# Hybrid recurrent decoder, two layers: a K 1024 product run out and back, S5 phases packed over partition halves, stores moved to GpSimd

## The chip, the core and the metric

The kernel runs on one core of a Trainium2 chip. The metric is the device time of one execution in microseconds. Timed runs and one profiled execution are given; the profiled one has a trace of every instruction.

## What is computed

Two layers of a decoder trunk for 512 prompt tokens and 64 sample tokens (8 sequences of 8), 576 columns in all, width 1024, in float32. Per layer:

```
h = RMSNorm(x);  P = h @ W_in                 (columns for four mixers and four gates)
A retention (4 heads), B Mamba-2 SSD (8 heads), C HGRN2 (4 heads), D S5 (32 groups of 16, 64 complex states)
m = sum_b sigmoid(P_gate_b) * (o_b @ W_branch_b);   x = x + RMSNorm(m @ W_out)
x = x + RMSNorm(relu(RMSNorm(x) @ W_1)^2 @ W_2)     (hidden width 4096)
```

It returns the outputs of both groups and the new recurrent states of every mixer (retention, SSD, convolution rows, HGRN2, S5), for each layer.

## The kernel before

Activations are kept transposed: features on the 128 partitions, tokens as columns, in two halves of 256 and 320 columns. Every dense product is made of three float32r products, (hi + lo) x (hi + lo) without lo x lo: `mm3` issues three matmuls for each 128 rows of K. A weight block (512 KB) is loaded by the SP queue into one of three `raw` buffers; ScalarE rounds it to `whi`, VectorE subtracts to get `wlo` (`wblock`), each in one of four buffers. So a fifth block is split only when TensorE has done with the first.

`dense` takes its output tiles in groups of four blocks. For a group it loads four blocks and runs all of its tiles for half 0, then all for half 1 (`order`). `hooks` are functions called ahead of a given tile of the last group: they put the norm of a half that is ready among the products that are still to run. `dense_turn` runs a first set of four tiles for half 0, the next set for half 0 and then half 1, and loads the first set again for half 1; it joins one product to the next, when half 1 of the input is not ready yet.

After the out-projection (`out_proj`, 8 tiles, K 1024, two groups) come `post` (norm of the result, added to `x`) and `norm` (the input of the FFN), for each half: squares on ScalarE, their sums and the scaling on VectorE, the sum over partitions on TensorE. `HK` places them: half 0's at tiles 0, 1 and 2 of half 1 in the last group, half 1's at tiles 1, 2 and 5 of the FFN's `dense_turn`. The FFN (`ffn`) takes the hidden width in eight chunks of 512: `up(c)` makes the chunk (relu, square, split into hi and lo), and the second product adds it into `y`, with K 512 and two tiles to a block. With the eighth chunk of layer 0 come the post-norm and layer 1's first norm, at the places `HM` and, for half 1, at `HN` in the `dense_turn` of layer 1 (four S5 tiles, then four of retention's first head).

S5 is run from tables that `s5_build` makes once per layer, on VectorE for the most part: groups of 16 channels in eight steps of four (`o`), each with an input table (`m2`), an output table (`cw`) and phases (`ph`, powers of the complex decay over 64 steps, from the power tables `w` and `E`), stored to DRAM (`tabd`) and loaded later. The 64 states stand on the partitions twice, as rows 0 to 63 and 64 to 127. Layer 0's tables are made beside the first mixer (retention), layer 1's beside layer 0's last merge. The places come from `SCHED`, a string with one letter per step, written out by hand.

All new states are stored by the SP queue, which also carries every load. A queue runs in order: a store waits there for its data, and what is behind it waits too. GpSimd has 16 memsets (HGRN2's `at` and `ats`) and four constants to write, and nothing else.

The order within an engine is made when the kernel is built: a planner goes through the operations with a cost model and gives each engine the ready operation that stands first in the written program; a buffer's next user waits for the last use of the one before. What the hardware does later than the plan thought, it does in that order still.

Of the kernel before, what the change touches and what calls it, by code (L numbers as in the profile page):

```python
# [40 lines left out]
FP = (0,4,7)  # L41
HN = (1,4,5)
HK = (0,1,2,1,2,5)
HM = (0,4,6)
HL = (0,5)
# [4 lines left out]
class Kernel:  # L50
# [586 lines left out]
    def out_proj(self, l, p, m, x):  # L637

        w = self.io["w_out"][l]
        y = [self.ytile(hf, "y") for hf in range(2)]  # L640
        h = []

        def take(k):
            return lambda ps, hf: self.act(y[hf][:, k], ps)

        post = lambda hf: lambda: self.post(y[hf], hf, p["g_post_mix"], x)
        norm = [self.norm(x, hf, p["g_pre_ffn"], "h", h) for hf in range(2)]
        step = lambda hf: lambda: next(norm[hf], None)
        self.dense(w, [(128 * k, take(k)) for k in range(8)], m, hooks=self.hooks(HK[:3], post(0), step(0), 1))
        return h, self.hooks(HK[3:], post(1), step(1))  # L650
# [11 lines left out]
    def ffn(self, l, p, h, rest, x, nxt, u1):  # L662
# [34 lines left out]
        if nxt is None:  # L697
            rows, done = self.last_rows(x[0], y[0], p["g_post_ffn"]), [0, 4]

            def tiles(k=None):  # L700

                if k is None:
                    self.store_x(x, 1)
                    done[1] = 8
                else:
                    done[0] += 1
                while done[1] and done[0]:
                    next(rows)
                    done[0] -= 1
                    done[1] -= 1  # L710
            order, hooks, end = (1, 0), {(0, HL[0]): [post(1)], (0, HL[1]): [tiles]}, None
        else:
            order, hooks = (0, 1), self.hooks(HM, post(0), step(0), 1)
            end = self.hooks(HN, post(1), step(1))
# [4 lines left out]
        for c in range(8):  # L719
            if c == 7 and nxt is None:  # L720
                next(rows)
            if c > 1:
                us.append(up(c))
                self.dense(w1, us[c][1], h)
            u = us[c][0]
            ua = [[(u[hf][0][:, i], u[hf][1][:, i]) for i in range(4)] for hf in range(2)]
            jobs = [(128 * k, take2(c, k)) for k in range(8)]
            if c < 7:
# [183 lines left out]
    def mixer_ret(self, l, p, h, res, turn):  # L912
        out, wi = [], self.io["w_in"][l]
        for hd in range(4):
# [26 lines left out]
            g = GAMMA[hd]  # L941
# [25 lines left out]
            for c in range(1, 4):  # L967
                self.stt(S[:, c], S[:, c - 1], g ** 128, pu[:, 128 * c:128 * c + 128], OP.mult, OP.add)
            self.nc.sync.dma_start(self.io["ret_prompt"][l, 0, hd], S[:, 3])

# [39 lines left out]
    def mixer_hg(self, l, p, h, res):  # L1010
        out, wi = [], self.io["w_in"][l]
        for hd in range(4):
# [107 lines left out]
            self.nc.sync.dma_start(self.io["hgrn_prompt"][l, 0, hd], S[:, 3])  # L1120
            o, sq = self.f([128, T], name="o"), self.f([128, T], name="osq")
# [16 lines left out]
            for i in range(2):  # L1138
                ps = self.pm()
                self.outer(ps, kts, vm[i])  # L1140
                for b in range(4):
                    c = NP + 8 * (4 * i + b) + 7
                    self.stt(st[i][:, b], st[i][:, b], eg[:, c:c + 1], ps[:, 128 * b:128 * b + 128], OP.mult, OP.add)
                self.nc.sync.dma_start(self.io["hgrn_sample"][l, 4 * i:4 * i + 4, hd].rearrange("b d e -> d b e"), st[i])
            rs = self.rowstat([sq], 1.0 / 128)
# [116 lines left out]
    def mixer_ssd(self, l, p, h, res):  # L1262
# [12 lines left out]
        for g in range(2):  # L1275
# [26 lines left out]
            for pr in range(2):  # L1302
# [29 lines left out]
                self.act(sp, ps[:, :128])  # L1332
                nc.sync.dma_start(io["ssd_prompt"][l, 0, h0:h0 + 2].rearrange("h p n -> (h p) n"), sp)

# [49 lines left out]
                for i in range(2):  # L1384
                    ps = self.pm()
                    self.outer(ps, xes, vm[i])
                    for b in range(4):
                        self.stt(st[i][:, b], st[i][:, b], dt["esm"][:, q, 4 * i + b:4 * i + b + 1],
                                 ps[:, 128 * b:128 * b + 128], OP.mult, OP.add)
                    nc.sync.dma_start(io["ssd_sample"][l, 4 * i:4 * i + 4, h0:h0 + 2].rearrange("b h p n -> (h p) b n"), st[i])  # L1390
            sq = [self.f([128, T], name="ssq") for _ in range(2)]
# [7 lines left out]
        for q in range(2):  # L1399
# [4 lines left out]
            self.act(r, ps[:27])  # L1404
            nc.sync.dma_start(io["conv_prompt"][l, 0][:, 512 * q:512 * q + 512], r[:3])
            nc.sync.dma_start(io["conv_sample"][l].rearrange("b r f -> (b r) f")[:, 512 * q:512 * q + 512], r[3:])
        self.dump(f"o_ssd{l}", out)
# [13 lines left out]
    def s5_build(self, l):  # L1421
# [3 lines left out]
        if l == 0:  # L1425

            A = self.slots.tile([128, 2048], F32, name="s5ba", tag="yA", bufs=1)
            Bt = self.slots.tile([128, 2560], F32, name="s5bb", tag="yB", bufs=1)
            base = [A[:, 512 * i:512 * i + 512] for i in range(4)] + [Bt[:, 512 * i:512 * i + 512] for i in range(2)]
            w, t, dd = Bt[:, 1024:1472], Bt[:, 1472:1984], Bt[:16, 1984:2496]  # L1430
        else:
            base = [self.f([128, 512], name="s5base") for _ in range(6)]
            w, t, dd = (self.f([128, n], name="s5t") for n in (448, 512, 512))
            dd = dd[:16]
# [19 lines left out]
        for i, (c, n) in enumerate(zip(C, ("s5_c_re", "s5_c_im"))):  # L1454
# [13 lines left out]
        t4 = t[:, :128].rearrange("p (k g) -> p k g", k=4)  # L1468
        for e, k0 in ((E[1], 0), (E[0], 3)):
            self.V.memset(e[:, 0, 0], 1.0)  # L1470
            self.V.memset(e[:, 0, 1], 0.0)
            for k in range(3):
                n = 1 << k
                self.cmulb((e[:, n:2 * n, 0], e[:, n:2 * n, 1]), (e[:, :n, 0], e[:, :n, 1]),
                           (w[:, k0 + k:k0 + k + 1, 0].to_broadcast([128, n, 32]),
                            w[:, k0 + k:k0 + k + 1, 1].to_broadcast([128, n, 32])), t4[:, :n])
        C3 = [g3(c) for c in C]
# [3 lines left out]
        for o in range(8):  # L1481
# [21 lines left out]
            self.tt(cw, cw, tmp, OP.add)  # L1503
            ph4 = v(ph, "p (c g a b) -> p c g a b", c=2, g=4, a=8)
            ea = lambda c: E[0][:, :, c, gs].rearrange("p a g -> p g a")[:, :, :, None].to_broadcast([128, 4, 8, 8])
            eb = lambda c: E[1][:, :, c, gs].rearrange("p b g -> p g b")[:, :, None, :].to_broadcast([128, 4, 8, 8])
            self.cmulb((ph4[:, 0], ph4[:, 1]), (ea(0), ea(1)), (eb(0), eb(1)), v(tm3, "p (g a b) -> p g a b", g=4, a=8))
            yield
# [10 lines left out]
            self.dq.dma_start(self.taps[l][:, 4 * o:4 * o + 4, 128:], kt[:16].rearrange("p (g q) -> p g q", g=4))  # L1519
            for (b0, b1, _, _), t in zip(self.TABS, (m2, cw, ph)):  # L1520
                self.dq.dma_start(self.tabd[l, o, :, b0:b1], t)
            if o == 7:

# [33 lines left out]
    def mixer_s5(self, l, p, ud):  # L1557
# [121 lines left out]
        for c, n in enumerate(("s5_re", "s5_im")):  # L1679
            nc.sync.dma_start(io[n + "_sample"][l].rearrange("(i b) g p -> (b g) i p", i=2), r[:, :2, 64 * c:64 * c + 64])  # L1680
            nc.sync.dma_start(io[n + "_prompt"][l, 0], r[:32, 2, 64 * c:64 * c + 64])
        self.dump(f"o_s5{l}", out)
# [78 lines left out]
```

## Time and profile before

| | |
|---|---|
| median of 3 timed runs | 2729.14 us (2728.92 to 2735.39) |
| the profiled execution | 2728.35 us, span of its instructions 2726.5 us |
| TensorE (PE) busy | 2651.0 us, 97% |
| VectorE (DVE) busy | 1735.4 us, 64% |
| ScalarE (ACT) busy | 1155.4 us, 42% |
| GpSimd (POOL) busy | 5.2 us |
| moved by DMA | 278.95 MB, mean 102 GB/s |

A row of the profile names the line of the kernel, the engine, the operation and the tiles (output <- inputs). Where a helper issues an operation, the line is the helper's, so tiles tell more: L108 is every matmul, L90 every ScalarE operation, L93 every two-operand VectorE operation. `pd` is the PSUM of dense products, `pm` that of all others. "SPq" is the SP queue, issuing or waiting.

### The profile page before, as it was taken

To read this page: it belongs to the slowest core of one execution; us is meant where nothing else is said; L and a number is where in the kernel's file an instruction comes from. 1 tells how busy PE (TensorE), PEld (TensorE's weight loads), DVE (VectorE), ACT (ScalarE), POOL (GpSimd) and SP (SyncE) were. 2 spreads that over 40 slices of the span, in tenths; PEclk is the share of its full clock that TensorE was granted. 3 is DMA by queue.
4 is the path that set the end of the run, shared out by engine and by line. 5 is a ranking of instruction groups with operands and counts; after the bars stand their busy time and mean duration, and the time that the engine had idled before them with its cause. 6 is when DMAs were issued, how large, how long until landed. Compare 5 with 4: busy or idle time off the path is not lost.

```text
span 2726.5 us, 48170 instructions
## 1 busy us (share of the span) xinstructions
PE 2651.0 (97%) x19498; PEld 2580.0 (95%) x19498; DVE 1735.4 (64%) x3806; ACT 1155.4 (42%) x2233; POOL 5.2 (0%) x20
## 2 busy tenths in 40 slices
PE   8989999999998999999989999999999999999998
PEld 8878999999998989999989999999999999999998
DVE  7797677867769483444485567777767546444445
ACT  5444554543532363322354554544434335423223
POOL 0000000000000000000000000000000000000000
PEclk9998999999999999999999999999999999999999
DMA  6445333332543533223244343333334323322221
GB/s 192 111 146 146 96 99 90 84 103 77 144 102 125 172 86 101 74 82 93 73 117 119 81 107 94 89 94 107 95 92 133 117 76 90 97 86 77 86 86 51
DMA packets 450540, 278.95 MB, mean 102 GB/s; under 512 B 58344, under 2 KB 430626, under 8 KB 449294
## 3 DMA queue, kind: packets, MB, share of 16 engines
q1 hardware_dynamic: 450318, 275.88, 35.9%
q8 instruction: 153, 2.51, 0.4%
q14 instruction: 69, 0.57, 0.1%
HBM read 235.20 MB, written 44.82 MB: 103 GB/s over the span
## 4 chain that ended last, share of the span: by engine, by line
PE 88%; DVE 7%; ACT 2%; DMA 2%; issue 1%; SPq 0%; DVEq 0%; ACTq 0%
PE pd L108 74%; PE pm L108 12%; PE pm L112 2%; DVE s5o L93 1%; DVE s5ob L93 1%; ACT whi L90 1%; DVE y L102 1%; DVE wlo L93 1%; DMA raw<-w_in 0%; DMA raw<-w_ff 0%; DMA s5tab<-tabd 0%; SPq L1446 0%; DVE x L93 0%; DVE nt L102 0%; DVE y L93 0%
## 5 line engine op out<-in xcount | busy, mean ns | idle before, releaser
L108 PE MATMUL pd<-hh,whi 128*128 128x256 f32 (+1 forms) x3584 | 1074.8, 301 | 16.7 <-ACT rv L90 7.2
L108 PE MATMUL pd<-hh,wlo 128*128 128x256 f32 (+1 forms) x3584 | 1072.5, 300 | 2.8 <-DVE wlo L93 2.8
L108 PE MATMUL pd<-hl,whi 128*128 128x256 f32 (+1 forms) x3584 | 1071.4, 300 | 0.8 <-DVE hl L93 0.7
L108 PEld LDWEIGHTS pd<-hh,whi 128*128 128x128 f32 x3584 | 686.2, 192 | 24.0 <-ACT rv L90 7.4
L90 ACT ACTIVATE whi<-raw 128x1024 fp32r<-128x1024 f32 x352 | 372.1, 1059 | 768.2 <-PE pd L108 690.6
L108 PEld LDWEIGHTS pd<-hh,wlo 128*128 128x128 f32 x3584 | 686.9, 192 | 5.8 <-DVE wlo L93 3.6
L93 DVE TENSOR_TENSOR wlo<-raw,whi 128x1024 fp32r<-128x1024 f32 x352 | 428.9, 1223 | 412.1 <-ACT whi L90 402.7
L108 PEld LDWEIGHTS pd<-hl,whi 128*128 128x128 f32 x3584 | 686.6, 192 | 3.6 <-DVE hl L93 1.3
L93 DVE TENSOR_TENSOR y<-y,pd 128x256 f32<-128x256 f32 (+1 forms) x224 | 100.9, 452 | 144.2 <-PE pd L108 143.8
L108 PE MATMUL pd<-obh,wlo 128*128 128x320 f32 (+1 forms) x512 | 153.5, 300 | 0.0
L108 PE MATMUL pd<-obh,whi 128*128 128x320 f32 (+1 forms) x512 | 152.7, 298 | 0.7 <-DVE gt L102 0.7
L108 PE MATMUL pd<-obl,whi 128*128 128x320 f32 (+1 forms) x512 | 152.4, 298 | 0.0
L108 PE MATMUL pd<-uh,whi 128*128 128x320 f32 (+1 forms) x512 | 151.6, 296 | 0.0
L108 PE MATMUL pd<-uh,wlo 128*128 128x320 f32 (+1 forms) x512 | 151.6, 296 | 0.0
L108 PE MATMUL pd<-ul,whi 128*128 128x320 f32 (+1 forms) x512 | 151.6, 296 | 0.0
L108 PEld LDWEIGHTS pd<-obh,whi 128*128 128x128 f32 x512 | 97.2, 190 | 1.5 <-DVE gt L102 1.0
L108 PEld LDWEIGHTS pd<-obh,wlo 128*128 128x128 f32 x512 | 97.0, 190 | 1.4 <-issue 0.8
L108 PEld LDWEIGHTS pd<-obl,whi 128*128 128x128 f32 x512 | 97.1, 190 | 0.3
L108 PEld LDWEIGHTS pd<-uh,whi 128*128 128x128 f32 x512 | 97.2, 190 | 0.0
L108 PEld LDWEIGHTS pd<-ul,whi 128*128 128x128 f32 x512 | 97.2, 190 | 0.0
L108 PEld LDWEIGHTS pd<-uh,wlo 128*128 128x128 f32 x512 | 97.2, 190 | 0.0
L90 ACT ACTIVATE rl<-pd 128x320 f32<-128x320 f32 (+1 forms) x128 | 50.9, 401 | 100.2 <-PE pd L108 100.2
(439 smaller groups left out, 4324.1 us busy)
## 6 DMA issues: line engine op xcount, KB each, us to landing
raw<-w_in SPq DMA_DIRECT2D x164, 512.0 KB
raw<-w_ff SPq DMA_DIRECT2D x136, 512.0 KB
raw<-w_branch SPq DMA_DIRECT2D x32, 512.0 KB
s5tab<-tabd SPq DMA_DIRECT2D x32, 256.0 KB
raw<-w_out SPq DMA_DIRECT2D x16, 512.0 KB
s5tab<-tabd SPq DMA_DIRECT2D x16, 288.0 KB
st<-state_ret SPq DMA_DIRECT2D x16, 256.0 KB
ret_sample<-st SPq DMA_DIRECT2D x16, 256.0 KB
```

The source lines that it names most:

```text
L90: self.S.activation(out, in_, func, **k)
L93: (e or self.V).tensor_tensor(out, a, b, op)
L102: (e or self.V).scalar_tensor_tensor(out, a, s, b, op0, op1)
L108: self.PE.matmul(out, lhsT=lhsT, rhs=rhs, start=start, stop=stop)
L112: self.PE.transpose(out, in_, self.ident[:k, :k])
```

## The change

- `dense_back` is new. It takes eight tiles of K 1024, four blocks at a time: half 0 of tiles 0 to 3, half 0 of 4 to 7, half 1 of 4 to 7, and then, with their blocks loaded and split again, half 1 of 0 to 3. The out-projections of both layers use it.
- In layer 0's FFN, chunk 6 of the second product waits for chunk 7. Both run as one product of K 1024 through `dense_back`, added into `y` once. `HM` and `HN` are other numbers.
- In `s5_build` the power tables hold groups 0 to 15 on partitions 0 to 63 and groups 16 to 31 on 64 to 127, at half the width. The phases of steps `o` and `o + 4` come from one computation, for `o` below 4, and are stored in four pieces.
- All stores of new states are issued by GpSimd (`nc.gpsimd.dma_start`) in place of SP.

```diff
-HN = (1,4,5)
+HN = (1,5,7)
-HM = (0,4,6)
+HM = (0,2,3)
...
+    def dense_back(self, w, jobs, a, hooks={}):
+        def go(js, ws, hf, n=0):
+            for i, (j, w2) in enumerate(zip(js, ws)):
+                if hf:
+                    for f in hooks.get(n + i, ()):
+                        f()
+                ps = self.dps(hf)
+                self.mm3(ps, w2, a, hf)
+                j[1](ps, hf)
+        js = jobs[:4], jobs[4:]
+        load = lambda js: [self.wblock(w, j[0])[0] for j in js]
+        go(js[0], load(js[0]), 0)
+        ws = load(js[1])
+        go(js[1], ws, 0)
+        go(js[1], ws, 1)
+        go(js[0], load(js[0]), 1, 4)
...
-        self.dense(w, [(128 * k, take(k)) for k in range(8)], m, hooks=self.hooks(HK[:3], post(0), step(0), 1))
+        self.dense_back(w, [(128 * k, take(k)) for k in range(8)], m, self.hooks(HK[:3], post(0), step(0)))
...
+            if c == 6 and nxt is not None:
+                continue
...
+            if c == 7 and nxt is not None:
+                ub = [[(us[6][0][hf][0][:, i], us[6][0][hf][1][:, i]) for i in range(4)] for hf in range(2)]
+                self.dense_back(w2[3072:], jobs, [ub[hf] + ua[hf] for hf in range(2)], hooks)
...
-        self.cp(w[:, 0, 0], M[:, 3])
-        self.cp(w[:, 0, 1], M[:, 4])
+        for r in range(2):
+            self.cp(w[64 * r:64 * r + 64, 0], M[64 * r:64 * r + 64, 3:5, 16 * r:16 * r + 16])
...
-            self.cmulb((ph4[:, 0], ph4[:, 1]), (ea(0), ea(1)), (eb(0), eb(1)), v(tm3, "p (g a b) -> p g a b", g=4, a=8))
+            if o < 4:
+                ...
+                self.cmulb((ph4[:, 0], ph4[:, 1]), (ea(0), ea(1)), (eb(0), eb(1)),
+                           v(tm3, "p (g a b) -> p g a b", g=4, a=8))
...
+            if o < 4:
+                b0, b1 = self.TABS[2][:2]
+                for r in range(2):
+                    for u in range(2):
+                        self.dq.dma_start(self.tabd[l, o + 4 * r, 64 * u:64 * u + 64, b0:b1], ph[64 * r:64 * r + 64])
...
-                self.nc.sync.dma_start(self.io["ret_sample"][l, 4 * i:4 * i + 4, hd].rearrange("b d e -> d b e"), st[i])
+                self.nc.gpsimd.dma_start(self.io["ret_sample"][l, 4 * i:4 * i + 4, hd].rearrange("b d e -> d b e"), st[i])
...
```

The last two lines stand for every store of a state: retention, HGRN2, SSD, convolution rows and S5.

## Rows read from the trace of the kernel before

**Rows 1.** Busy time by stage: stretch, length, PE, PEld, DVE, ACT, POOL, clock, DMA.
```profile
95.00:245.00 150.00, 134.49 (x902) 122.79 (x901) 132.48 (x329) 71.81 (x139) 0.14 (x1) 0.89 0.46 127
245.00:815.00 570.00, 567.06 (x4265) 552.05 (x4263) 408.95 (x930) 263.40 (x529) 2.35 (x7) 0.99 0.38 103
815.00:905.00 90.00, 81.19 (x592) 75.88 (x591) 86.81 (x221) 26.98 (x48) 0.00 (x0) 0.98 0.44 139
...
940.00:1010.00 70.00, 63.09 (x444) 59.91 (x444) 55.53 (x121) 42.27 (x90) 0.00 (x0) 0.98 0.34 91
...
1365.00:1441.00 76.00, 64.67 (x439) 61.95 (x438) 59.00 (x133) 37.51 (x79) 0.00 (x0) 0.91 0.35 101
...
2271.00:2321.00 50.00, 47.43 (x338) 44.57 (x338) 44.92 (x103) 33.34 (x74) 0.00 (x0) 1.00 0.31 85
```
**Rows 2.** PE in order of time, 194 to 204 us: start, duration, [idle before].
```profile
197.15 0.63 PE L112 MATMUL pm<-c_ident,s5oa 128*128 128x128 f32 x4 [2.19 <-DVE s5oa L93]
...
203.47 0.58 PE L108 MATMUL pd<-hh,whi 128*128 128x256 f32 x1 [2.47 <-DVE rq L93]
```
**Rows 3.** DVE groups by form, 95 to 245 us: busy us, mean ns, idle before.
```profile
L93 DVE TENSOR_TENSOR s5ob<-s5bb 128x256 f32<-128x256 f32 x32 | 18.8, 610 | 0.0
...
L93 DVE TENSOR_TENSOR s5ob<-s5ob 128x256 f32<-128x256 f32 x16 | 6.7, 417 | 0.0
...
L93 DVE TENSOR_TENSOR s5bb<-s5bb 128x32 f32<-128x32 f32 x42 | 5.9, 187 | 0.0
...
L93 DVE TENSOR_TENSOR s5bb<-s5bb 128x128 f32<-128x128 f32 x12 | 3.3, 287 | 0.0
```
**Rows 4.** PE in order of time, 830 to 850 us: first and last wait of six.
```profile
832.21 0.41 PE L108 MATMUL pd<-obh,whi 128*128 128x320 f32 x1 [0.69 <-DVE gt L102]
...
849.19 0.39 PE L108 MATMUL pd<-hh,wlo 128*128 128x256 f32 x1 [1.35 <-DVE wlo L93]
```
**Rows 5.** PE in order of time, 860 to 900 us.
```profile
874.35 0.63 PE L112 MATMUL pm<-c_ident,s5o 128*128 128x128 f32 x4 [0.74 <-DVE s5o L93]
```
**Rows 6.** What PE waited for, 940 to 1010 us: total, times, longest.
```profile
PE pm L108 <- DVE sq L93: 2.9, 2, 1.7
PE pd L108 <- ACT hh L90: 2.1, 2, 1.6
PE pd L108 <- ACT whi L90: 1.0, 1, 1.0
PE pd L108 <- DVE wlo L93: 0.8, 1, 0.8
```
**Rows 7.** ACT in order of time, 928 to 944 us (layer 0's out-projection).
```profile
940.11 2.94 ACT L90 ACTIVATE whi<-raw 128x1024 fp32r<-128x1024 f32 x3
```
**Rows 8.** ACT in order of time, 2249 to 2254 us (layer 1's out-projection).
```profile
2249.15 1.06 ACT L90 ACTIVATE whi<-raw 128x1024 fp32r<-128x1024 f32 x1 [2.54 <-PE pd L108]
2250.11 0.42 ACT L90 ACTIVATE y<-pd 128x320 f32<-128x320 f32 x1
```
**Rows 9.** What PE waited for, 1365 to 1441 us.
```profile
PE pd L108 <- ACT rv L90: 7.2, 1, 7.2
PE pd L108 <- DVE y L93: 2.0, 1, 2.0
PE pd L108 <- ACT hh L90: 1.7, 1, 1.7
```
**Rows 10.** DVE groups by form, 1365 to 1441 us.
```profile
L93 DVE TENSOR_TENSOR wlo<-raw,whi 128x1024 fp32r<-128x1024 f32 x9 | 10.8, 1222 | 1.8 <-ACT whi L90 1.8
...
L102 DVE SCALAR_TENSOR_TENSOR nt<-y,par,rs 128x256 f32<-128x256 f32 x8 | 3.4, 480 | 0.0
...
L93 DVE TENSOR_TENSOR hl<-nt,hh 128x256 fp32r<-128x256 f32 x8 | 2.9, 421 | 0.0
```
**Rows 11.** SP's issues of a state store (L992): minimum, median, maximum ns.
```profile
L992 SPq DMA_DIRECT2D ret_sample<-st x16: 373/388/412, 95.0 to 1587.7; - x16
```
**Rows 12.** SP's issues of an S5 load (L1446), the same columns.
```profile
L1446 SPq DMA_DIRECT2D s5b<-s_b_re x4: 645/1519/4348, 60.6 to 796.9; - x4
```

More of the change, by code (lines that the diff above doesn't have):

```diff
@@ L712, in ffn @@
         else:
-            order, hooks = (0, 1), self.hooks(HM, post(0), step(0), 1)
+            order, hooks = (0, 1), self.hooks(HM, post(0), step(0))
             end = self.hooks(HN, post(1), step(1))
@@ L968, in mixer_ret @@
                 self.stt(S[:, c], S[:, c - 1], g ** 128, pu[:, 128 * c:128 * c + 128], OP.mult, OP.add)
-            self.nc.sync.dma_start(self.io["ret_prompt"][l, 0, hd], S[:, 3])
+            self.nc.gpsimd.dma_start(self.io["ret_prompt"][l, 0, hd], S[:, 3])
             o = self.f([128, T], name="o")
@@ L1119, in mixer_hg @@
                          OP.mult, OP.add)
-            self.nc.sync.dma_start(self.io["hgrn_prompt"][l, 0, hd], S[:, 3])
+            self.nc.gpsimd.dma_start(self.io["hgrn_prompt"][l, 0, hd], S[:, 3])
             o, sq = self.f([128, T], name="o"), self.f([128, T], name="osq")
@@ L1332, in mixer_ssd @@
                 self.act(sp, ps[:, :128])
-                nc.sync.dma_start(io["ssd_prompt"][l, 0, h0:h0 + 2].rearrange("h p n -> (h p) n"), sp)
+                nc.gpsimd.dma_start(io["ssd_prompt"][l, 0, h0:h0 + 2].rearrange("h p n -> (h p) n"), sp)
                 st = []
@@ L1389, in mixer_ssd @@
                                  ps[:, 128 * b:128 * b + 128], OP.mult, OP.add)
-                    nc.sync.dma_start(io["ssd_sample"][l, 4 * i:4 * i + 4, h0:h0 + 2].rearrange("b h p n -> (h p) b n"), st[i])
+                    nc.gpsimd.dma_start(io["ssd_sample"][l, 4 * i:4 * i + 4, h0:h0 + 2].rearrange("b h p n -> (h p) b n"), st[i])
             sq = [self.f([128, T], name="ssq") for _ in range(2)]
@@ L1404, in mixer_ssd @@
             self.act(r, ps[:27])
-            nc.sync.dma_start(io["conv_prompt"][l, 0][:, 512 * q:512 * q + 512], r[:3])
-            nc.sync.dma_start(io["conv_sample"][l].rearrange("b r f -> (b r) f")[:, 512 * q:512 * q + 512], r[3:])
+            nc.gpsimd.dma_start(io["conv_prompt"][l, 0][:, 512 * q:512 * q + 512], r[:3])
+            nc.gpsimd.dma_start(io["conv_sample"][l].rearrange("b r f -> (b r) f")[:, 512 * q:512 * q + 512], r[3:])
         self.dump(f"o_ssd{l}", out)
@@ L1428, in s5_build @@
             Bt = self.slots.tile([128, 2560], F32, name="s5bb", tag="yB", bufs=1)
-            base = [A[:, 512 * i:512 * i + 512] for i in range(4)] + [Bt[:, 512 * i:512 * i + 512] for i in range(2)]
-            w, t, dd = Bt[:, 1024:1472], Bt[:, 1472:1984], Bt[:16, 1984:2496]
-        else:
-            base = [self.f([128, 512], name="s5base") for _ in range(6)]
-            w, t, dd = (self.f([128, n], name="s5t") for n in (448, 512, 512))
+            base = [A[:, 512 * i:512 * i + 512] for i in range(4)] + [Bt[:, 256 * i:256 * i + 256] for i in range(2)]
+            w, t, dd = Bt[:, 1024:1248], Bt[:, 1472:1984], Bt[:16, 1984:2496]
+        else:
+            base = [self.f([128, 512], name="s5base") for _ in range(4)]
+            e = self.f([128, 512], name="s5base")
+            base += [e[:, :256], e[:, 256:]]
+            w, t, dd = (self.f([128, n], name="s5t") for n in (224, 512, 512))
             dd = dd[:16]
@@ L1474, in s5_build @@
                 self.cmulb((e[:, n:2 * n, 0], e[:, n:2 * n, 1]), (e[:, :n, 0], e[:, :n, 1]),
-                           (w[:, k0 + k:k0 + k + 1, 0].to_broadcast([128, n, 32]),
-                            w[:, k0 + k:k0 + k + 1, 1].to_broadcast([128, n, 32])), t4[:, :n])
+                           (w[:, k0 + k:k0 + k + 1, 0].to_broadcast([128, n, 16]),
+                            w[:, k0 + k:k0 + k + 1, 1].to_broadcast([128, n, 16])), t4[:, :n])
         C3 = [g3(c) for c in C]
@@ L1503, in s5_build @@
             self.tt(cw, cw, tmp, OP.add)
-            ph4 = v(ph, "p (c g a b) -> p c g a b", c=2, g=4, a=8)
-            ea = lambda c: E[0][:, :, c, gs].rearrange("p a g -> p g a")[:, :, :, None].to_broadcast([128, 4, 8, 8])
-            eb = lambda c: E[1][:, :, c, gs].rearrange("p b g -> p g b")[:, :, None, :].to_broadcast([128, 4, 8, 8])
-            self.cmulb((ph4[:, 0], ph4[:, 1]), (ea(0), ea(1)), (eb(0), eb(1)), v(tm3, "p (g a b) -> p g a b", g=4, a=8))
+            if o < 4:
+                ph4 = v(ph, "p (c g a b) -> p c g a b", c=2, g=4, a=8)
+                ea = lambda c: E[0][:, :, c, gs].rearrange("p a g -> p g a")[:, :, :, None].to_broadcast([128, 4, 8, 8])
+                eb = lambda c: E[1][:, :, c, gs].rearrange("p b g -> p g b")[:, :, None, :].to_broadcast([128, 4, 8, 8])
+                self.cmulb((ph4[:, 0], ph4[:, 1]), (ea(0), ea(1)), (eb(0), eb(1)),
+                           v(tm3, "p (g a b) -> p g a b", g=4, a=8))
             yield
@@ L1519, in s5_build @@
             self.dq.dma_start(self.taps[l][:, 4 * o:4 * o + 4, 128:], kt[:16].rearrange("p (g q) -> p g q", g=4))
-            for (b0, b1, _, _), t in zip(self.TABS, (m2, cw, ph)):
+            for (b0, b1, _, _), t in zip(self.TABS, (m2, cw)):
                 self.dq.dma_start(self.tabd[l, o, :, b0:b1], t)
+            if o < 4:
[3 more added lines that the diff above has]
+                        self.dq.dma_start(self.tabd[l, o + 4 * r, 64 * u:64 * u + 64, b0:b1], ph[64 * r:64 * r + 64])
             if o == 7:
@@ L1679, in mixer_s5 @@
         for c, n in enumerate(("s5_re", "s5_im")):
-            nc.sync.dma_start(io[n + "_sample"][l].rearrange("(i b) g p -> (b g) i p", i=2), r[:, :2, 64 * c:64 * c + 64])
-            nc.sync.dma_start(io[n + "_prompt"][l, 0], r[:32, 2, 64 * c:64 * c + 64])
+            nc.gpsimd.dma_start(io[n + "_sample"][l].rearrange("(i b) g p -> (b g) i p", i=2), r[:, :2, 64 * c:64 * c + 64])
+            nc.gpsimd.dma_start(io[n + "_prompt"][l, 0], r[:32, 2, 64 * c:64 * c + 64])
         self.dump(f"o_s5{l}", out)
```

6 lines of the change are left out of this document (3 added, 3 removed).

## The prediction

> **What bounds the kernel now.** I read the windows by stage first: length less TensorE's (PE's) busy time is what can be won in a stage, and the granted clock says what the busy time itself lost. From 245 to 815 us, the mixers of layer 0, PE is busy 567.06 of 570.00 us [rows 1]: no edit that acts there can gain more than 3 us, and a cost to PE there shows at once. The stages that the change touches are the loose ones [rows 1]: 95 to 245 (building layer 0's S5 tables beside retention) idles 150.00 - 134.49 = 15.5 us at clock 0.89, which is another 0.11 x 150 = 16 us of work at the low level (1.2 instead of 2.4 GHz); 815 to 905 (layer 1's tables beside the last merge) idles 8.8 us; 940 to 1010 (out-projection into FFN, layer 0) 6.9 us; 1365 to 1441 (FFN into layer 1) 11.3 us at clock 0.91, 7 us more; 2271 to 2321 (out-projection into FFN, layer 1) 2.6 us. Together 45 us idle. In all of them VectorE (DVE) is nearly full: 132.48 of 150, 86.81 of 90, 55.53 of 70 [rows 1].
>
> Next the waits of PE in each stage, to see whose lateness it is. In the first, PE waits for DVE [rows 2]; in the second too [rows 4, 5]; in the out-projection for sums of squares, for `hh` and once for weight splits [rows 6]; at the end of the FFN for `rv` 7.2 us, for `y` 2.0 and for `hh` 1.7 [rows 9]. Those three are one story: DVE does the post-norm and pre-norm of the first half after the last matmul of that half's partner, so the second half's norm comes late, and the evacuations that free PSUM stand behind it.
>
> **Packed S5 phases.** Per layer, 32 multiplies of 128x256 take 18.8 us and their 16 adds 6.7 us [rows 3]: 25.5 us, of which half (groups 4 to 7) go: 12.75, or 3.2 us for each of four groups. The power tables halve in width: 42 operations of 128x32 take 5.9 us and 12 of 128x128 3.3 us [rows 3], thus 0.14 and 0.28 us each; 96 columns fewer cost 0.14 us less, 1.4 ns a column. Taking 16 columns off 42, 32 off 12 (128x64) and 64 off 12 saves 0.9 + 0.5 + 1.1 = 2.5 us; I take 2, since I do not trust the slope at the short end. DVE thus loses 15 us per layer. What of it lies on the path?
> - Layer 0: the phases of groups 4 and 5 stand on DVE just before the three waits of PE between 194 and 203 us, 2.19 + 1.36 + 2.47 = 6.0 us (first and last of three in [rows 2]). Two groups are 6.4 us, so 6.0 goes. Group 6 lies under unbroken PE work, nothing. The last group and the tables touch small waits: 2. Sum 8. Some of the low clock might come back as well, and the planner will put other work forward; I let these cancel. Ends: 2 (only tables and trifles) and 15.5 (all idle time) plus 8 (half of the clock loss).
> - Layer 1: the six waits from 832 to 849 us, 7.1 us (first and last in [rows 4]), come before group 4: only the 2 us of the tables help there. Behind it stand 0.74 [rows 5] and two smaller ones, 1.4 in all; I take 1. Sum 3; ends 1 and 8.8.
> - The phase stores become 16 pieces instead of 8 per layer. They cost 8 more issues on SP, at the 0.39 us of a store [rows 11] 3 us over 150, beside what follows, so nothing.
>
> **Stores by GpSimd.** 88 stores (44 a layer, counted in the code) leave SP: 88 x 0.388 = 34 us of issue [rows 11] and the waits before them. SP is the queue of weight loads, yet PE waits for no load in the stages where the stores are (567 of 570 us busy) [rows 1], so the gain is nothing, bounded by those 3 us in layer 0. The cost: no row shows a DMA issued by GpSimd. The nearest are on SP: 0.388 us for such a store [rows 11] and 4.35 us for the longest issue of many small pieces [rows 12]. I take the first; on an otherwise empty engine even the second, 44 x 4.35 = 191 us in a layer, is hidden. Queued behind a store on GpSimd are only HGRN's memsets. The Trainium skill ("SBUF — State Buffer", "Who interferes with whom") says that a DMA from GpSimd has its descriptors written by the engine itself, and that it and a VectorE copy or tensor-scalar in a two-port mode lock each other out for whole instructions, which speaks against the move; no run here shows it so far. By that rule the sum could lose a store's length on DVE for every store, which the last rival prices from rows; by the rows it loses nothing.
>
> **Out-projection back, both layers.** Half 0 now runs all 8 jobs, then half 1 runs 4 to 7 and 0 to 3 with blocks 0 to 3 loaded and split again. Post-norm and pre-norm of half 0 get 8 jobs of half 1 as cover instead of 4 (24 matmuls each). In layer 0 the waits for `sq` (2.9) and `hh` (2.1) [rows 6] should go, and with the longest the low clock: 0.02 x 70 = 1.4. Gain 6.4. Added: 4 blocks, each a `wlo` of 1.22 us on DVE [rows 10], in the stretch where the norms run: 8 x 1.22 = 9.8, plus the half's norms. DVE is just about full there, so I give back 1. The turn: with four split buffers, the fifth block is split only when the first is free. Layer 0 shows what that costs when `whi` is queued behind the last evacuation (940.11 us [rows 7]): 1.0 + 0.8 us of PE [rows 6]. Layer 1 shows it free, with `whi` between two evacuations [rows 8]. There was one such turn, now there are two; I charge the second 1.8. Net 6.4 - 1 - 1.8 = 3.6, taken as 4. In layer 1, 2.6 idle less one turn at 1.8: 1. Ends: -2 and 7, -1 and 2.6.
>
> **FFN of layer 0.** Chunks 6 and 7 become one product of K 1024: the same matmuls, 16 fewer adds into `y`, 12 blocks instead of 8. Half 0's post-norm begins when half 0 is done and has 8 jobs of 24 matmuls as cover rather than 8 of 12. What then leaves the stretch after the last matmul: `nt` and `hl` of half 0, 3.4 + 2.9 = 6.3 us of DVE [rows 10], the wait for `y` (2.0) and for `hh` (1.7). The new hook places put three of retention's evacuations ahead of the second half's norm, so the 7.2 us for `rv` can go with these 6.3 and the better order [rows 9]. All three: 10.9; the low clock that followed them, 0.09 x 76 = 7 of which more than half fell on idle time: 3. That makes 14. Two turns at 1.8 cost 3.6 and four re-splits 4 x 1.22 = 4.9 of DVE, of which I charge 1.4. Gain 9; ends 3 and 14. The extra 12 x 0.5 = 6 MB of weights are under PE work in all three places.
>
> **Sum.** 8 + 3 + 4 + 1 + 9 = 25 us. The profiled execution took 2728.35 us (span 2726.5 and 1.85 around it): 2703.4. The median of the runs is 0.8 above it: **2704 us**.
>
> **Rivals.** A difference under 0.3% (8 us) cannot be told from no change; 2721 and 2737 are the bounds.
> - *The turns cost.* For it: [rows 7] stalls in exactly this pattern; against: [rows 8]. If all six turns stall 1.8 us and the engine falls to the low clock after each, as in the first stage, where clock loss is about as large as idle time [rows 1], 21 us are paid where I charged 7: 2704 + 14 = 2718, still faster, with 2714 if two are free.
> - *The phases were hidden.* DVE is in order and the planner packs other work (`rq`, `rs`, weight splits) into the room, so PE waits as before; the tables alone count: 2 + 1 instead of 11, 2712. For it: in layer 1 the waits do stand before the removed work [rows 4]. Together with the first: 2722 to 2726, no measurable change.
> - *More comes back.* All 45 us of idle time and half of the clock loss, 11 us, return, less some 16 us for turns and re-splits: 40 us, 2688. For it: DVE is the cause in every stage [rows 2, 4, 6, 9]; against: it stays the fullest, (132.48 - 15) of 142 us or 83% in the first stage.
> - *Stores on GpSimd block DVE* (slower). Each of a layer's 44 stores stops DVE while it is issued. DVE has 570 - 409 = 161 us free in layer 0's mixers [rows 1], 3.7 us a store; from there on DVE is the bound. At 4.35 us [rows 12] it is 191 - 161 = 30 us over, 60 for two layers, and 60 - 25 = 35 slower: 2764. For it: no row shows the operation. Against: it needs the top of the bound at every store.
> - *Nothing of it takes effect* cannot be: the planner takes the written order as priority, and the removed operations are gone.
>
> **Chances.** Forecast 0.50 (its own range 2696 to 2712, the parts' errors of some 3 to 4 us each); turns 0.15; phases hidden 0.14; both 0.09; more 0.06; GpSimd 0.06. Faster is the forecast, the two single rivals and the better case less 0.02 that spills: 0.83; same is both rivals and that spill: 0.11; slower 0.06. The range leaves out the GpSimd case, part of the better one and of both together: 2686 to 2722.
>
> **What would show it.** DVE's phase rows at 16 multiplies and 8 adds per layer; PE busy over 140 of 150 us in the first stage; no wait of PE for `rv` or `y` at the end of the FFN; at most two waits for `whi` or `wlo` behind each turn; PE still busy 567 of 570 in the mixers. The prediction is wrong if PE's idle time in those five stages falls by less than 15 us, or if DVE shows waits or longer operations beside GpSimd's stores.

## The result, and the profile after

The changed kernel takes a median of 2695.95 us (2692.95 to 2700.79), the kernel before 2729.17 us beside it; the ratio is 0.9872, 95% interval 0.9854 to 0.9889, so some 33 to 35 us faster. The profiled execution took 2696.73 us with a span of 2695.0 us: 31.5 us of span less. The forecast was 2704 (25 us); the result is on the better side of it, inside the range and 0.05 us under the forecast's own 2696 to 2712.

Busy time by stage, after, in stretches that answer to [rows 1] (length, PE, PEld, DVE, ACT, POOL, clock, DMA). Layer 0's out-projection (the fourth line) is taken from its first matmul on, since its first turn now comes early in it; counted that way the kernel before idles the same 6.9 us:

```profile
95.00:239.00 144.00, 133.83 (x940) 122.24 (x940) 122.16 (x311) 73.55 (x145) 7.84 (x12) 0.95 0.48 130
239.00:809.00 570.00, 565.29 (x4248) 550.78 (x4248) 408.77 (x926) 261.56 (x523) 23.56 (x39) 0.99 0.38 103
809.00:895.00 86.00, 80.60 (x580) 74.89 (x578) 74.67 (x196) 26.57 (x47) 0.00 (x0) 0.96 0.49 144
904.00:1000.00 96.00, 93.08 (x679) 90.27 (x678) 69.35 (x141) 57.12 (x115) 0.00 (x0) 1.00 0.44 128
1348.00:1416.00 68.00, 67.10 (x472) 64.56 (x471) 58.18 (x122) 38.59 (x77) 0.00 (x0) 1.00 0.47 132
2236.00:2286.00 50.00, 49.85 (x358) 48.18 (x357) 44.70 (x95) 33.46 (x72) 0.00 (x0) 1.00 0.44 121
```

Length less PE's busy time is 10.2, 5.4, 2.9, 0.9 and 0.15 us in the five loose stages (all but the second line): 19.5 where 45 stood, so 25.6 us less. Over the whole execution PE idles 50.3 us instead of 75.5, 25.2 less; the other 6 us of the 31.5 are busy time of the same 19498 matmuls, shorter by the clock. The last two stages have nothing left to win, and the clock of the last three is 1.00. The mixers idle 4.7 us instead of 2.9. The difference is one wait, the first load of an S5 table (what PE waited for, 239 to 809 us):

```profile
PE pm L108 <- DMA s5tab<-tabd: 1.8, 1, 1.8
```

All nine profiles with packed phases show it at that place, with 1.1 to 3.3 us, and none of the five without: PE now comes to the first use of a table before the table has landed.

What PE waited for in layer 0's out-projection (905 to 999 us), then at the end of its FFN (1348 to 1416 us), against [rows 6, 9]: total, times, longest. Layer 0's out-projection, where the 1.6 us and the longer of the two others stand at the first turn, at 917 to 919 us:

```profile
PE pm L108 <- issue: 1.6, 1, 1.6
PE pd L108 <- DVE wlo L93: 1.1, 2, 0.6
```

The end of the FFN:

```profile
PE pd L108 <- ACT hh L90: 0.5, 1, 0.5
PE pd L108 <- DVE hl L93: 0.3, 1, 0.3
```

The waits for `rv` (7.2) and `y` (2.0) are gone, those for `sq` and `hh` nearly so (the 1.6 us put down to "issue" end 0.3 us after DVE's sum of squares). VectorE's groups by form in the first stage of after, against [rows 3]:

```profile
L93 DVE TENSOR_TENSOR s5ob<-s5bb 128x256 f32<-128x256 f32 x16 | 9.5, 620 | 0.0
...
L93 DVE TENSOR_TENSOR s5bb<-s5bb 128x16 f32<-128x16 f32 x42 | 5.0, 162 | 0.0
...
L93 DVE TENSOR_TENSOR s5ob<-s5ob 128x256 f32<-128x256 f32 x8 | 3.3, 416 | 0.0
...
L93 DVE TENSOR_TENSOR s5bb<-s5bb 128x64 f32<-128x64 f32 x12 | 2.5, 216 | 0.0
...
L93 DVE TENSOR_TENSOR s5bb<-s5bb 128x32 f32<-128x32 f32 x12 | 2.0, 178 | 0.0
```

12.7 us of phases are gone (18.8 + 6.7 less 9.5 + 3.3), as worked out; the narrow tables saved 0.9 + 0.8 + 0.6 = 2.3 us (the last from 12 operations of 128x64, 2.6 us before) where 2 was taken.

To see where the time came from, I compare when PE reaches the same matmul in the two traces:

| PE reaches | before | after | stage's change | forecast |
|---|---|---|---|---|
| first matmul of layer 0's first merge (`obh`) | 277.64 | 271.47 | -6.2 | -8 |
| first of out-projection 0 (`mhh`) | 913.98 | 904.09 | -3.7 | -3 |
| first of FFN 0 for half 1 (`hh`, 320 columns) | 1002.67 | 988.63 | -4.2 | -4 |
| first of layer 1 for half 1 (`hh`, 320) | 1434.55 | 1406.08 | -14.4 | -9 |
| first of out-projection 1 | 2234.05 | 2206.30 | +0.7 | 0 |
| first of FFN 1 for half 1 | 2319.54 | 2288.14 | -3.6 | -1 |
| end | 2726.49 | 2694.96 | -0.1 | 0 |

### The profile page after: what moved, and what is told of

Read it like the earlier page. It is cut to its first block, busy times and chain, and to the rows that moved or that the text cites. A ratio compares the mean times of both kernels' runs of the same rounds, so it can differ in the third digit from the quotient of the medians.

```text
span 2695.0 us, 48304 instructions
## 1 busy us (share of the span) xinstructions
PE 2644.7 (98%) x19498; PEld 2574.5 (96%) x19498; DVE 1718.8 (64%) x3754; ACT 1165.8 (43%) x2245; POOL 64.3 (2%) x108
## 3 DMA queue, kind: packets, MB, share of 16 engines
q1 hardware_dynamic: 436902, 267.50, 35.3%
## 4 chain that ended last, share of the span: by engine, by line
PE 91%; DVE 5%; ACT 2%; DMA 1%; issue 1%; SPq 1%; DVEq 0%; ACTq 0%
PE pd L108 76%; PE pm L108 12%; PE pm L112 2%; DVE s5o L93 1%; ACT whi L90 0%; DVE y L102 0%; DMA s5tab<-tabd 0%; DMA raw<-w_in 0%; DVE sq L93 0%; DVE x L93 0%; SPq L1472 0%; DVE wlo L93 0%; DVE s5ob L93 0%; SPq L1560 0%; DMA ssds<-ssd_a_log 0%
## 5 line engine op out<-in xcount | busy, mean ns | idle before, releaser
L90 ACT ACTIVATE whi<-raw 128x1024 fp32r<-128x1024 f32 x364 | 384.8, 1059 | 749.9 <-PE pd L108 661.7
L93 DVE TENSOR_TENSOR wlo<-raw,whi 128x1024 fp32r<-128x1024 f32 x364 | 442.7, 1222 | 399.9 <-ACT whi L90 390.2
L93 DVE TENSOR_TENSOR y<-y,pd 128x256 f32<-128x256 f32 (+1 forms) x208 | 93.7, 452 | 138.8 <-PE pd L108 138.7
L90 ACT ACTIVATE gt<-pd 128x320 f32<-128x320 f32 (+1 forms) x128 | 51.5, 402 | 105.3 <-PE pd L108 94.5
```

The costliest lines, as they stand in the source:

```text
L90: self.S.activation(out, in_, func, **k)
L93: (e or self.V).tensor_tensor(out, a, b, op)
```

## The experiments

Executions of one program differ by several microseconds (the stores alone gave 2720.75 to 2732.03 us in 12 runs), so a stage is judged over several profiles. "Ratio" is to the kernel before on the same chip.

| kernel | median us | before | ratio | 95% |
|---|---|---|---|---|
| one_s5 | 2720.70 | 2728.10 | 0.9972 | 0.9962 to 0.9983 |
| one_out | 2721.86 | 2728.10 | 0.9980 | 0.9970 to 0.9991 |
| one_ffn | 2715.23 | 2728.10 | 0.9955 | 0.9940 to 0.9969 |
| one_pool | 2727.77 | 2728.10 | 1.0000 | 0.9991 to 1.0009 |
| whole (the change) | 2691.07 | 2727.08 | 0.9867 | 0.9852 to 0.9882 |
| all_sp | 2701.05 | 2727.08 | 0.9906 | 0.9889 to 0.9922 |
| turns3 | 2692.32 | 2727.08 | 0.9870 | 0.9844 to 0.9895 |
| join_only | 2701.39 | 2727.08 | 0.9903 | 0.9883 to 0.9924 |
| s5_pool | 2715.44 | 2727.00 | 0.9960 | 0.9947 to 0.9972 |
| pool_ret | 2691.28 | 2727.00 | 0.9864 | 0.9849 to 0.9878 |
| tables_pool | 2699.03 | 2727.00 | 0.9897 | 0.9880 to 0.9913 |
| hooks_only | 2720.07 | 2727.63 | 0.9975 | 0.9963 to 0.9986 |

### Each part alone

**one_s5**: the `s5_build` hunks alone.

```diff
+            if o < 4:
+                ph4 = v(ph, "p (c g a b) -> p c g a b", c=2, g=4, a=8)
...
```


> The kernel before with the packed S5 phases alone. Theory (the idle time of TensorE that the removed work caused goes, part by part, and the parts add): 9.9 us faster, 6.2 from the start to the first merge matmul and 3.7 to the out-projection, as the two traces show between the same landmarks; about 2719 us. Rival (the phases were hidden, and what the changed kernel gained there came from SP being free of the stores): only the 3 us of the narrower power tables, 2726.

Measured 7.6 us by the ratio, between the two and nearer the theory. In the profile the first merge matmul came at 272.64, 5.0 us earlier and not 6.2 to 8, and the tables of layer 1 gave 4.5.

**one_out**: `dense_back` in the out-projections alone.

```diff
-        self.dense(w, [(128 * k, take(k)) for k in range(8)], m, hooks=self.hooks(HK[:3], post(0), step(0), 1))
+        self.dense_back(w, [(128 * k, take(k)) for k in range(8)], m, self.hooks(HK[:3], post(0), step(0)))
```


> The kernel before with the out-projections alone run out and back. Theory (parts add, turns are free): 7 to 8 us faster, some 4 in each layer; about 2721.5. Rival (a turn costs 1.8 us, as the forecast charged for the second one, and is free in the changed kernel only because no stores stand on SP): 4 to 5 faster, 2724.5, with waits of TensorE for whi or wlo behind both turns.

Measured 5.5 us (2.5 to 8): the time does not decide. The busy time by stage does, layer 0's from the first matmul of the out-projection on, layer 1's as in [rows 1]. First the kernel before, then one_out twice:

```profile
914.00:1010.00 96.00, 89.09 (x638) 85.68 (x638) 60.72 (x130) 49.16 (x104) 0.00 (x0) 0.98 0.35 101
914.00:1010.00 96.00, 93.07 (x679) 90.26 (x678) 69.56 (x141) 57.39 (x116) 0.00 (x0) 1.00 0.46 130
2271.00:2321.00 50.00, 49.84 (x361) 48.06 (x361) 42.09 (x88) 33.20 (x69) 0.00 (x0) 1.00 0.41 116
```

Idle falls from 6.9 to 2.9 and from 2.6 to 0.2 us with the stores still on SP. The first turn costs PE 2.2 us, as in the changed kernel; the way back stalls nowhere. Between the matmuls of the first table the two stages are 4.2 and 3.6 us shorter, together the theory's 7 to 8.

**one_ffn**: the K 1024 product with `HM` and `HN` alone (`ffn`'s hunks of the change).

```diff
-HN = (1,4,5)
+HN = (1,5,7)
-HM = (0,4,6)
+HM = (0,2,3)
...
+                self.dense_back(w2[3072:], jobs, [ub[hf] + ua[hf] for hf in range(2)], hooks)
```


> The kernel before with the last two chunks of layer 0's second product alone in one of K 1024, out and back, with the new hook places. Theory (turns and re-splits are covered, the waits for rv, y and hh go with the low clock behind them): 14 us faster, 2715. Rival (the forecast's charge of 5 us for two turns and four re-splits is right and the rest came from the other parts): 9 faster, 2720, with waits for whi or wlo of 3 to 4 us in sum at the turns.

Measured 12.3 us (8 to 16), nearer the theory. Its profile shows no wait for `whi` or `wlo` between 1365 and 1430 us, only 0.5 us for `hh` and 0.3 for `hl`; PE reaches layer 1's half 1 27.45 us after the last `u1` matmul instead of 36.50.

**one_pool**: the stores alone.

```diff
-                self.nc.sync.dma_start(self.io["ret_sample"][l, 4 * i:4 * i + 4, hd].rearrange("b d e -> d b e"), st[i])
+                self.nc.gpsimd.dma_start(self.io["ret_sample"][l, 4 * i:4 * i + 4, hd].rearrange("b d e -> d b e"), st[i])
...
```


> The kernel before with the stores alone moved to GpSimd. Theory: no change, 2729 within 2 us, since TensorE is 99% busy where the stores are and waits for no load. Rival 1 (SP freed of 34 us of issue brings loads earlier, and that is what made the turns free): 4 to 6 us faster. Rival 2 (the stores on GpSimd hold up VectorE, hidden in the whole change by its gains): slower by 3 us or more, with longer VectorE operations beside the stores.

No change: the theory. A store holds GpSimd about twice as long as its issue held SP [rows 11], here in the profile of one_pool (GpSimd's groups by form: busy us, mean ns, idle before):

```profile
L992 POOL DMA_DIRECT2D ret_sample<-st x16 | 12.1, 756 | 43.3 <-DVE st L102 42.3 <-issue 0.8
```

PE is busy 567.09 of 570 us in this kernel's mixers too, so nothing waits for that.

### The parts together

**whole**: the changed kernel once more.

> The changed kernel once more, beside the three that follow and with as many runs as the parts had. Theory (the parts add): the parts alone came to 7.6 + 5.5 + 12.3 + 0 = 25 us by their ratios, so 2703. Rival (they help each other, through a shared state of the queues or of the clock): the 33 us of the first comparison stand, 2695.

The rival: 36 us (32 to 40), not 25. The parts alone do not add up to the change.

**all_sp**: the change without its fourth part.

```diff
-            self.nc.gpsimd.dma_start(self.io["ret_prompt"][l, 0, hd], S[:, 3])
+            self.nc.sync.dma_start(self.io["ret_prompt"][l, 0, hd], S[:, 3])
...
```


> The changed kernel with its stores of states back on SP. Theory (stores cost and give nothing, alone or with the rest): as the changed kernel, within 2 us. Rival (with twelve blocks reloaded SP becomes tight, and the stores taken off it are what the parts alone lacked): 6 to 8 us slower than the changed kernel.

10 us slower than the changed kernel on the same chip, with ranges that do not touch (2698.88 to 2702.92 against 2689.39 to 2691.95). So the three other parts add (7.6 + 5.5 + 12.3 = 25.4, measured 26), and the stores, worth nothing alone, are worth 10 in company. The rival's size was nearly right (6 to 8), its place wrong: the traces of the two differ before the first merge (9.4 us) and by 1.3 us or less anywhere else. PE in order of time, the two waits near 195 us and the first merge matmul ([rows 2] has the waits before), in all_sp:

```profile
195.64 0.63 PE L112 MATMUL pm<-c_ident,s5oa 128*128 128x128 f32 x4 [3.65 <-DVE s5oa L93]
198.01 1.86 PE L108 MATMUL pm<-s5ob,s5oa 128*16 128x128 f32 x8 [1.75 <-DVE s5ob L93]
...
275.98 0.28 PE L108 MATMUL pd<-obh,whi 128*128 128x256 f32 x1
```

And in whole:

```profile
192.15 0.39 PE L108 MATMUL pd<-hh,whi 128*128 128x256 f32 x1 [1.63 <-DVE rq L93]
...
197.18 1.03 PE L108 MATMUL pm<-s5ob,s5oa 128*16 128x128 f32 x8 [1.46 <-DVE s5ob L93]
...
266.59 0.28 PE L108 MATMUL pd<-obh,whi 128*128 128x256 f32 x1
```

Busy time from 186 to 210 us, in all_sp:

```profile
186.00:210.00 24.00, 18.60 (x122) 16.94 (x121) 20.58 (x38) 11.40 (x20) 0.00 (x0) 0.86 0.33 108
```

And in whole:

```profile
186.00:210.00 24.00, 20.91 (x155) 19.96 (x155) 22.37 (x42) 12.87 (x23) 0.00 (x0) 1.00 0.45 134
```

In the same 24 us PE issued 122 matmuls and 155. With the stores on SP its order has the four transposes of `s5oa` behind the 840th dense matmul of layer 0, before DVE has made them; PE waits 3.65 us, and the mean clock of these 24 us is 0.86. With packed phases and retention's stores on GpSimd the planner put them behind the 862nd, 22 matmuls later, and that wait is gone. (By the `pd<-hh` and `pd<-hl` matmuls ahead of them: 840 also in every kernel without packed phases, one_pool among them, and in one_s5; 862 in s5_pool, pool_ret, turns3, join_only, whole and the first profile of the change, whose order on PE, DVE, ACT and SP is one and the same up to the first merge.)

What such a wait costs is mostly clock. Busy time from the first transposes of `s5oa` to those behind the 960th dense matmul, in whole, all_sp and one_s5:

```profile
126.93:213.41 86.48, 80.01 (x593) 74.75 (x592) 76.71 (x162) 42.33 (x79) 4.09 (x6) 1.00 0.57 159
125.18:219.67 94.49, 87.10 (x594) 81.29 (x592) 77.31 (x162) 42.35 (x79) 0.00 (x0) 0.91 0.52 146
128.00:218.99 90.99, 82.61 (x594) 76.44 (x593) 77.26 (x162) 42.28 (x79) 0.00 (x0) 0.96 0.54 152
```

All six profiles with the later transposes take 86.4 to 86.5 us here, at clock 1.00. all_sp idles 7.4 us instead of 6.5, 0.9 more, but is 8.0 us longer: the clock fell to its low level of 1.2 GHz behind the wait (0.50 from 197 to 201 us) and in three stretches ahead of it. one_s5, with the same order of PE, fell only behind the wait, and is 4.5 us longer than whole. So the place seems to account for some 4.5 us; why all_sp's clock fell three times more is not shown.

**s5_pool**: before with the packed phases and the stores, the two edits shown above.

> The kernel before with the packed phases and the stores on GpSimd, nothing else. Theory (the two help each other in the first 277 us: the order there is the changed kernel's, and its first merge matmul came at 266.6 to 271.5 us in four profiles against 272.6 and 276.0 with packed phases and SP stores): 0.994, 15 to 18 us faster than before. Rival (parts add; the 10 us between the changed kernel and the one with SP stores were luck of the runs): 0.9972, 8 us.

11 us (8 to 14), against 7.6 of the phases alone: the ratio lies between the two. The profile has the theory's order, with the first merge matmul at 267.50 us.

**pool_ret**: the change, with only retention's stores on GpSimd.

```diff
-            self.nc.gpsimd.dma_start(self.io["hgrn_prompt"][l, 0, hd], S[:, 3])
+            self.nc.sync.dma_start(self.io["hgrn_prompt"][l, 0, hd], S[:, 3])
...
```


> The changed kernel with only retention's stores (24 of 88) on GpSimd, all others back on SP. Theory (what the stores on GpSimd give, they give in the first stage, where retention's 12 of layer 0 stood in SP's order among the table stores and weight loads; the order of TensorE and VectorE is the changed kernel's until the mixers): as the changed kernel, 0.987, within 3 us. Rival (all 88 count, or the reloaded blocks of the products that run back are what SP gets to earlier): as the one with all stores on SP, 0.9906, 10 us slower.

As the changed kernel (2691.28 us): the theory. Sixty-four of the 88 moved stores give nothing that can be measured. Over the profiles with packed phases (tables_pool, below, left out), the first merge matmul came at 266.38, 266.59, 267.50, 268.12, 269.70 and 271.47 us with retention's stores on GpSimd, at 272.64 and 275.98 with them on SP: 268.3 and 274.3 in the mean, 6 us of the 10. Part of this is scatter from the start of the kernel: the six, alike in order, reach the first `s5oa` transposes anywhere from 124.9 to 130.4 us. Counted from there to the first merge they take 139.3 to 141.6 us, the two with stores on SP 144.6 and 150.8, the five profiles without packed phases 150.6 to 151.4.

**tables_pool**: the change, with the stores of the S5 tables and taps on GpSimd too.

```diff
-                self.dq.dma_start(self.tabd[l, o, :, b0:b1], t)
+                self.nc.gpsimd.dma_start(self.tabd[l, o, :, b0:b1], t)
...
```


> The changed kernel with the stores of the S5 tables and taps on GpSimd as well (32 phase pieces, 32 tables and 16 tap stores leave SP, which keeps the loads). Theory (SP's order, in which a weight load stands behind a store that waits for VectorE, is what costs in the first stage): 2 to 5 us faster than the changed kernel, first merge matmul at 265 us or before. Rival (only the planner's order of VectorE changed with the stores, and SP itself delayed nothing): no change, or slower by the 0.55 to 0.75 us that a store takes on GpSimd where a table's way to DRAM is waited for.

Not the theory: 8 us slower than the change, and more than the rival's 0.55 to 0.75. The transposes are back behind the 840th matmul, though retention's stores are on GpSimd, and the stretch from the first transposes to the first merge takes 150.2 us (the first merge matmul came at 283.61, in the slowest of the six runs, which reached those transposes only at 133.4). What PE waited for, 95 to 262 us:

```profile
PE pm L108 <- DMA s5tab<-tabd: 3.3, 1, 3.3
PE pd L108 <- DVE rq L93: 2.8, 2, 1.6
PE pm L108 <- DVE at L102: 2.4, 1, 2.4
```

So "SP freed" is not what pays by itself. The first line is in part the rival's: the way of a table through DRAM, 3.3 us where the other packed profiles wait 1.1 to 2.2. The rest goes with the place that the planner gives to work that DVE makes: slow with the transposes behind the 840th matmul, on whichever queue retention's stores stand, and fast in the six with 862.

### Inside the FFN term

**turns3**: the change, with a third turn in all three products.

```diff
-        go(js[1], ws, 1)
-        go(js[0], load(js[0]), 1, 4)
+        go(js[0], load(js[0]), 1)
+        go(js[1], load(js[1]), 1, 4)
```


> The changed kernel with a third turn in each of the three products that run out and back: half 1 runs blocks 0 to 3 and then 4 to 7, all eight loaded and split again, so three turns and twelve blocks more split. Theory (turns and re-splits are free): within 2 us of the changed kernel. Rival (1.8 us a turn, and a share of the 12 x 1.22 us of splits, as the forecast charged): 5.4 us to 10 us slower, with waits for whi or wlo at each turn.

1.2 us slower than the change: the theory, with 12 more blocks split at 1222 ns each. The four runs spread over 16 us, so the stages of the first table say more: FFN 0 and layer 1's out-projection lost nothing (417.5 and 81.1 us, 417.9 and 81.9 in whole), and only layer 0's out-projection did (58.98 us from its first to its last matmul instead of 56.96), to waits for `sq` of 2.8 us and not for weights.

**join_only**: the change, with the K 1024 product not run back.

```diff
-                self.dense_back(w2[3072:], jobs, [ub[hf] + ua[hf] for hf in range(2)], hooks)
+                self.dense(w2[3072:], jobs, [ub[hf] + ua[hf] for hf in range(2)], order, hooks)
```
(and the places `HM` for half 1.)

> The changed kernel with the product of K 1024 run by the old routine: two groups of four blocks, each for half 0 and then for half 1, eight blocks and one turn; the norm of half 0 has four tiles of 24 matmuls behind it instead of eight. Theory (the longer cover is what removes the waits for rv, y and hh): 5 to 9 us slower than the changed kernel, the waits back behind the last matmul of the feed-forward. Rival (the 16 additions that went and the new hook places do it, the way back only costs): as the changed kernel or 2 us faster.

10 us slower by the medians; 5.3 us of it in the place that the edit touches (33.20 us from the last `u1` matmul to layer 1's half 1 instead of 27.91). The rest is in no one stage: the two profiles differ by 6.9 us in all. PE's waits, 1348 to 1416 us:

```profile
PE pd L108 <- ACT hh L90: 4.5, 2, 2.6
PE pd L108 <- DVE hl L93: 0.3, 1, 0.3
```

The theory by size, though only the wait for `hh` is back: joining the chunks without the way back leaves half 0's norm late. `rv` is not among the waits, which the next one explains.

**hooks_only**: before, with the new `HN`.

```diff
-HN = (1,4,5)
+HN = (1,5,7)
```


> The kernel before with the later places of the second half's norm alone (tiles 1, 5 and 7 of the turn into layer 1 instead of 1, 4 and 5). Theory (the 7.2 us wait for rv stands there because that norm's steps are put ahead of retention's evacuations; later places remove it, whatever the product before does): the wait for rv gone, 4 to 6 us faster, 2722. Rival (the first half's norm is what is late; without the cover of the out-and-back product the same delay turns up as a wait for hh or for the sums of squares): within 2 us of before, with waits of the same sum under other names.

6.8 us faster (4 to 10): the theory, from two numbers of a tuple. PE's waits from 1365 to 1441 us, against [rows 9]:

```profile
PE pd L108 <- ACT hh L90: 3.8, 2, 2.1
PE pd L108 <- DVE y L93: 2.0, 1, 2.0
PE pd L108 <- DVE hl L93: 0.3, 1, 0.3
```

`rv` is gone; of its 7.2 us 2.1 come back as a second wait for `hh`, and the stage is 5.2 us shorter (31.30 for 36.50). The product run out and back takes the rest, `y` and both `hh`.

## Why the prediction was right, and what was mis-sized

The direction, the places and the causes held: VectorE was late in each loose stage, and the work that went was the work named. Of the signs, the rows of the phases, the missing waits for `rv` and `y`, the two short waits behind a turn and the idle time (25.6 us less, 15 asked for) came as said; PE busy 133.8 of 144 us in the first stage (92.9%) is just under the 140 of 150, and the mixers show 565 of 570 us where 567 was said: PE does wait for a load there, a table's, 1.8 us. One sign of being wrong did come, longer DVE operations beside GpSimd's stores, but twice in the kernel and 0.5 us in all (last section). Step by step:

- **Phases of layer 0, 8.** 6.2 between the two first profiles, 9 between the means of all (277.4 for the five profiles without packed phases, 268.3 for the six with them and retention's stores on GpSimd). The size was right in part by luck: I took the removed DVE work off PE's waits one for one and let the low clock cancel. Of the three waits of [rows 2], 6.0 us, two are left, of 1.63 and 1.45 us, so 3 went. From the first `s5oa` transposes to the first merge the first pair is 9.8 us apart, of which idle time is 3.9 (13.4 to 9.5); the rest is the clock, 0.90 before and 0.96 after. Alone the phases gave 3 (277.4 to 274.3), with the transposes where PE waits for them; the other 6 came when the stores moved.
- **Stores by GpSimd, 0.** Right alone (one_pool), wrong in company: 10 us by the medians, 6 of them seen in the first stage. The step that failed is "PE waits for no load in the stages where the stores are, so the gain is nothing": it asked only what the queue costs on the chip, and not what the planner does with an edited queue. That the order is the cause, and not the queue itself, rests on the counted places in the traces and on tables_pool, slow with the old place and retention's stores on GpSimd; the new place with those stores on SP was not tried.
- **FFN, 9.** Measured 14.4 in the first pair, 12.3 alone. The gross 14 was about right; what was mis-sized is the 5 taken off for turns and re-splits. In the FFN they cost nothing (turns3). ScalarE in order of time shows why, in layer 0's out-projection after: the first turn, then the second.

```profile
916.54 2.94 ACT L90 ACTIVATE whi<-raw 128x1024 fp32r<-128x1024 f32 x3
...
935.01 1.06 ACT L90 ACTIVATE whi<-raw 128x1024 fp32r<-128x1024 f32 x1 [1.48 <-PE pd L108]
935.97 0.42 ACT L90 ACTIVATE y<-pd 128x320 f32<-128x320 f32 x1
...
938.53 1.06 ACT L90 ACTIVATE whi<-raw 128x1024 fp32r<-128x1024 f32 x1 [0.59 <-PE pd L108]
...
940.41 0.42 ACT L90 ACTIVATE y<-pd 128x320 f32<-128x320 f32 x1
```

  At the first the three `whi` still stand in a row behind the last evacuation, as in [rows 7], and PE waits 2.2 us beside it (1.6 and 0.6); at the second each follows its own matmul's end, as in [rows 8], and PE does not wait. So I charged the pattern of [rows 7] to turns that follow [rows 8]. And the three waits of [rows 9] were not one story: `rv` went with the hook places alone (hooks_only), `y` with the joined product (join_only), `hh` only with the way back.
- **Out-projections, 4 and 1.** 4.2 and 3.6. Layer 1's turns were free, and its stretch lost nearly all of its idle time.
- **Layer 1's tables, 3.** 3.7 in the first pair, 4.4 over all profiles. The two rows where nothing was forecast sum to 0.6 us slower.
- **Rivals.** The turns rival falls with turns3. "Phases hidden" is half true of the phases alone. "More comes back" (2688) was as near as the forecast (the result lies 8 us from either): 25.6 of the 45 us idle came back, and the clock is at 1.00 in the two FFN and out-projection stages of layer 0 that stood at 0.91 and 0.98. The GpSimd rival is below.

By whole runs the parts and the pair that we ran (s5_pool 11, one_out 5.5, one_ffn 12.3) sum to 29 against 36. By stages, where the scatter of the rest of the kernel drops out, the sum is 35. Means in us over all profiles that have the part and all that have not (turns3 is left out of the last three rows, hooks_only and join_only, which have a part of the edit, out of FFN 0):

| stretch of PE | without | with | gain | forecast |
|---|---|---|---|---|
| first `s5oa` transposes to first merge (with: the later transposes) | 151.0 | 140.5 | 10.5 | 8 |
| from there to out-projection 0 | 636.2 | 631.8 | 4.4 | 3 |
| out-projection 0 to FFN 0, half 1 | 88.7 | 84.8 | 4.0 | 4 |
| FFN 0 to layer 1, half 1 | 430.0 | 417.7 | 12.3 | 9 |
| out-projection 1 to FFN 1, half 1 | 85.5 | 81.9 | 3.6 | 1 |

So the parts add by stage, once the stores have changed the order. Still open is why, without that order, the packed phases took 144.6 us for the first stretch in one profile and 150.8 in another.

## What to carry to other kernels

Price a removed operation on the engine that waits, and then look at whether the order can use the gap: where a planner lays the order, parts of a change can be worth nothing alone and 10 us in company, so test them together as well as apart. A wait can cost more in clock than in idle time, so compare both. Extra turns and reloads were free here where the conversion of their weights stood between evacuations and not behind them. Before building a larger rearrangement, try the places of the hooks: two numbers gave 7 of the 12 us.

## What was not expected of the hardware

A store on GpSimd does hold VectorE up, but in this kernel only in one kind of operation. S5's gate scaling, `s5g`, is a TENSOR_SCALAR from SBUF to SBUF, and its last one in each layer falls beside a store of S5's states. All 16 by minimum, median and maximum ns, first and last start, in the profile before:

```profile
L99 DVE TENSOR_SCALAR s5g<-s5g x16: 287/306/332, 782.2 to 2159.3; 128x256 f32<-128x256 f32 x8, 128x320 f32<-128x320 f32 x8
```

And in the one after:

```profile
L99 DVE TENSOR_SCALAR s5g<-s5g x16: 278/296/571, 774.8 to 2131.6; 128x256 f32<-128x256 f32 x8, 128x320 f32<-128x320 f32 x8
```

320 ns without a store, 571 and 567 ns beside one (at 786.94 us, with GpSimd's 0.73 us store from 786.65 on, and at 2131.58). The other operations that a store overlaps did not grow: 142 TENSOR_TENSOR and SCALAR_TENSOR_TENSOR instructions in the profile after took 1 and 2 ns less in the mean than the median of the same tiles and shape without a store, and the one COPY of 128x256 from SBUF to SBUF that meets a store (`s5a`, at 712.98 us) took 294 ns, its median. The Trainium skill ("SBUF — State Buffer", "Who interferes with whom") has this lock for the two-port modes, copies and TENSOR_SCALARs among them; the trace agrees for `s5g`, with a price of 0.25 us each time, and does not show in which mode an instruction ran. By that rule the last rival could have been real; here two operations meet a store, 0.5 us in all, and the 2764 needed 3.7 us at every one.
